# Three row blocks of scores in one stretch, the decays' products of two head pairs in one stretch, two later steps of groups: a hybrid decoder layer on one Trainium2 core

## The chip, the cores and the metric

The kernel runs on one core of one Trainium2 chip. The core has a matrix engine (PE in the profile, with its weight loads, PEld), a vector engine (DVE), a scalar engine (ACT), a general engine (POOL) and a sync engine (SP), which all run their own instruction queues in order and wait for each other by semaphores. The metric is the time of one execution on the device in microseconds (us), the median of several runs. Before the change it is 1290.15 us, the median of three runs (1289.37 to 1290.36).

## The reference

The input is x, 512 tokens of width 1024, and a memory of 256 tokens of the same width. The layer is a feed-forward half step, a mixer, a cross-attention into the memory, and a second feed-forward half step, each behind an RMS norm and added to x. All is in float32. The change lies in the mixer, which has two kinds of heads behind one input projection and ahead of one output projection:

```python
z, xbc, dt_raw, q, k, v = split_sizes(h @ w_in, IN_SIZES)
xbc = silu(causal_dwconv(xbc, conv_w, conv_b))          # 4 taps
# SSD: 16 heads of 64 in 4 groups, chunks of 128 tokens
decay = exp(where(causal, la_cum[l] - la_cum[s], -inf))
y_diag = einsum('bclsg,bclsgr,bcsgrp->bclgrp', cb, decay, xdt)
y_off = einsum('bclgn,bcgrpn,bclgr->bclgrp', cc, prev, exp(la_cum))
y = (y_diag + y_off + d_skip * xh) * silu(z)            # then an RMS norm by group
# differential attention: 8 heads, 2 components of 64, values of 128, query blocks of 128
p = softmax(q @ k.T * scale + bias, causal)             # for both components
o = (p[0] - lam * p[1]) @ v                             # then an RMS norm by head
out = concatenate([y_ssd, y_attn]) @ w_out
```

`y_diag` is what the tile `py` holds, and `y_off` what `pf` holds. A query block of row i sees the keys of blocks 0 to i alone, so its scores are 128 by 128(i+1).

## The kernel before

The whole layer is one program. Activations are kept with features on the partitions and 512 tokens along the free axis. Every float32 weight and activation is split into a high part and a low remainder (`split_into`, L153), and a product is made of three passes of matmuls: high by high, low by high, high by low. The dense projections are runs of 24 matmuls of 128x512, written `pq<-hnh,wh` and the like, into a bank of PSUM; the tile gets its name from what it holds (`pq`, `pk` queries and keys of a head, `pxbc` and `pz` inputs of the SSD groups, `pm` output projection, `pcv` values of the memory).

PSUM has eight banks here in two pools of four: `acc` for the dense projections, and `aux` for all that the heads and groups do beside them (`ps` scores, `pt` turned weights, `po` outputs of a head, `ptk` and `pot` two transposes of these, `pcb`, `pxt`, `pbt`, `pst`, `pf`, `py` and `nps`, `nrow` of a group). A new tile takes the bank that has been in use for the longest time, and its first matmul waits for the last reader of that bank.

The order of the work is set in two steps. A class `Order` runs generators: the dense projections step matmul by matmul, and the heads (`head`, L766) and groups (`group`, L928) are spawned beside them and resume when a clock, which every matmul moves on by an estimate of its time, has passed what they yielded. These delays stand in a table `W` (`hs` between the steps of a head, `gd`, `gt`, `gy`, `gq`, `gn` between those of a group). A scheduler of the framework then sets the order on PE, DVE and ACT from that program; the order of SP and POOL is that of the program.

In `head` (L766) the scores of the four row blocks are made by `scores`: for each block three passes over two components, each component a matmul on 64 of PE's rows (`64*128` in the profile), both at once, into a bank for each component. A read on DVE (L787, a custom operation that scales, adds the bias and keeps the minimum, followed by a small read of that minimum `mn`) and an exponential on ACT (L788) follow for each component. `combine(i)` makes the difference of the two components on DVE (L796, L798, L799), and `turn(j)` transposes the columns of key block j into `pt`, which is then split into `wt` on ACT and DVE. `po` sums the values, ACT copies it (`of`), and PE transposes it (`ptk`). Before the change a head runs `scores(3)`, `scores(2)` one step later, and `scores(1, 0)`, both into one pair of banks, one step after that.

In `group` (L928) the last part (from L982) runs twice, once for each pair of heads j: the decays come from a row on ACT (L989 to L993), then `pf` takes three matmuls and `py` eight, of 128x128, four chunks by two heads, each on 64 of PE's columns (`128*64` in the profile). DVE then makes `y` (L1008, L1009), and with `z` (L1017) the gated output, whose squares (`ysq`) go to a sum over tokens, an inverse root on POOL (`ncol`, L368) and back to a row (`nrow`). `decays(g + 1, j)` fetches the row for the next group into the tile that the group has just read. The taps of the convolution (L901) run on DVE beside that and are the last readers of a bank of `pxbc`.

## Time and profile before

| what | us |
| --- | --- |
| median of 3 runs | 1290.15 |
| the profiled execution | 1289.51 |
| its span, first to last instruction | 1287.7 |
| PE busy | 1275.9 (99%) |
| DVE busy | 969.3 (75%) |
| ACT busy | 708.2 (55%) |
| mixer with its heads and groups | about 375 to 840 of the span |
| PE busy from 375 to 840 | 464.38 of 465 |

A row of a timeline reads: start, duration, engine, line, operation, tile written and tiles read, rows by columns of PE that are used, shape and number of like instructions one after the other, and in brackets how long the engine had been idle and what it then waited for. Matmuls overlap their neighbours, so the time that one takes is best read from the starts of the rows. The clock of PE was granted at 0.997 of full speed over the execution.

### The profile page before, as it was taken

The page shows a single profiled execution, that of the slowest core. Times are in us where ns is not written, and L with a number is a line of the kernel's source. Part 1 is how long each engine was busy: PE and PEld are TensorE (multiplying, and loading weights), DVE is VectorE, ACT ScalarE, POOL GpSimd, SP SyncE. Part 2 cuts the span into 40 slices and gives each one's busy share as a digit, 9 for nine tenths or more (in the row PEclk, how much of TensorE's full clock was granted, in tenths as well). Part 3 has the DMA queues.
Part 4 walks back from the last instruction along what each step waited for, and adds up shares of the span by engine and source line. Part 5 has one row for each costly group of instructions (what it writes and reads, how often), then busy time and mean ns, then how long its engine had stood idle before and what let it go on. Part 6 is the DMA issues. An engine that isn't in the chain of part 4 may idle for free.

```text
span 1287.7 us, 20009 instructions
## 1 busy us (share of the span) xinstructions
PE 1275.9 (99%) x7673; PEld 1115.9 (87%) x7673; DVE 969.3 (75%) x1547; ACT 708.2 (55%) x1207; POOL 111.6 (9%) x135
## 2 busy tenths in 40 slices
PE   9999999999999999999999999999999999999996
PEld 7889998998988788877888878888899899989995
DVE  6988898788875786657768697546668878877886
ACT  7545564566654564446654566434475546545554
POOL 1001010002201011101102011020001000000000
PEclk9999999999999999999999999999999999999998
DMA  9468677789865436753376457593259776666662
GB/s 338 104 173 209 180 204 203 217 217 238 284 205 159 128 74 191 214 173 84 96 224 199 137 150 241 197 229 99 69 160 243 207 222 177 193 190 187 186 202 87
DMA packets 69695, 234.70 MB, mean 182 GB/s; under 512 B 8144, under 2 KB 9568, under 8 KB 69248
## 3 DMA queue, kind: packets, MB, share of 16 engines
q1 hardware_dynamic: 53504, 181.12, 41.9%
q0 software_dynamic: 13456, 45.67, 19.8%
q10 hardware_dynamic: 2640, 6.65, 1.6%
q8 instruction: 60, 0.98, 0.3%
q14 instruction: 35, 0.29, 0.1%
HBM read 231.25 MB, written 48.29 MB: 217 GB/s over the span
## 4 chain that ended last, share of the span: by engine, by line
PE 88%; issue 9%; ACT 1%; POOL 1%; DMA 1%; DVE 1%; POOLq 0%; DVEq 0%; ACTq 0%
PE qb L244 13%; PE pm L146 9%; PE qe L244 9%; PE qa L244 8%; PE ob L1328 7%; PE oa L1328 5%; PE oe L1328 4%; PE pk L146 3%; PE pv L146 3%; PE pq L146 3%; PE pcq L146 3%; PE pxbc L146 3%; PE pck L146 2%; PE pa L146 2%; PE pg L146 2%
## 5 line engine op out<-in xcount | busy, mean ns | idle before, releaser
L155 ACT ACTIVATE wh<-wr 128x1024 fp32r<-128x1024 f32 (+1 forms) x245 | 251.2, 1028 | 223.4 <-PE qe L244 31.0
L156 DVE TENSOR_TENSOR wl<-wr,wh 128x1024 fp32r<-128x1024 f32 (+1 forms) x245 | 290.0, 1186 | 74.6 <-ACT wh L155 60.2
L1308 ACT ACTIVATE wh<-wr 128x1024 fp32r<-128x1024 f32 (+1 forms) x74 | 72.8, 984 | 65.9 <-PE ob L1328 17.4
L1317 DVE TENSOR_TENSOR wl<-wr,wh 128x1024 fp32r<-128x1024 f32 (+1 forms) x74 | 82.7, 1126 | 12.9 <-ACT wh L1308 11.0
L788 ACT ACTIVATE ec<-ec,mn 128x512 f32<-128x512 f32 (+3 forms) x64 | 35.3, 554 | 21.9 <-DVE mn L787 21.9
L787 DVE CUSTOM_DVE_ANT_0 ec<-ps,bias 128x512 f32<-128x512 f32 (+3 forms) x64 | 28.1, 487 | 16.2 <-PE ps L146 16.1
L368 POOL TENSOR_TENSOR ncol<-nv,mhalf 128x4 f32<-128x4 f32 (+1 forms) x9 | 11.4, 1271 | 299.8 <-DVE nv L366 299.8
L901 DVE SCALAR_TENSOR_TENSOR conv<-pxbc,par,conv 128x511 f32<-128x511 f32 (+2 forms) x48 | 35.8, 745 | 1.9 <-ACT conv L897 1.3
L253 POOL DMA_DIRECT2D wr<-in_f2q x11 | 9.7, 879 | 306.1 <-DMA wr<-in_f2q 230.4
L146 PE MATMUL pxbc<-hnl,wh 128*128 128x512 f32 x128 | 35.6, 405 | 0.0
L146 PE MATMUL pxbc<-hnh,wh 128*128 128x512 f32 x128 | 34.7, 398 | 0.0
L146 PE MATMUL pxbc<-hnh,wl 128*128 128x512 f32 x128 | 32.5, 393 | 0.0
L456 DVE TENSOR_TENSOR gate<-qb,row 128x512 f32<-128x512 f32 x19 | 13.1, 692 | 20.3 <-PE qb L244 20.3
L146 PEld LDWEIGHTS pxbc<-hnh,wl 128*128 128x128 f32 x128 | 23.7, 188 | 5.2 <-issue 0.2
L146 PEld LDWEIGHTS pxbc<-hnl,wh 128*128 128x128 f32 x128 | 23.1, 188 | 4.9 <-issue 0.6
L146 PEld LDWEIGHTS pxbc<-hnh,wh 128*128 128x128 f32 x128 | 23.4, 189 | 4.6 <-issue 0.3
L253 POOL DMA_DIRECT2D wr<-in_f1q x16 | 14.0, 872 | 152.3 <-DVE wl L156 44.6
L457 ACT ACTIVATE gate<-gate 128x1024 f32<-128x1024 f32 x19 | 20.1, 1057 | 10.9 <-DVE gate L456 10.9
L146 PE MATMUL pv<-wh,hnh 128*128 128x512 f32 x64 | 25.4, 398 | 0.0
L146 PE MATMUL pv<-wh,hnl 128*128 128x512 f32 x64 | 25.1, 393 | 0.0
L155 ACT ACTIVATE s24h<-s 128x512 fp32r<-128x512 f32 x30 | 18.8, 627 | 9.0 <-DVE s L214 9.0
L155 ACT ACTIVATE s31h<-s 128x512 fp32r<-128x512 f32 x30 | 18.7, 624 | 7.3 <-DVE s L212 4.2
(472 smaller groups left out, 3506.3 us busy)
## 6 DMA issues: line engine op xcount, KB each, us to landing
wr<-in_f2q SPq DMA_DIRECT2D x44, 512.0 KB, 4.3
wr<-in_f1q SPq DMA_DIRECT2D x40, 512.0 KB, 4.7
wr<-in_f1b SPq DMA_DIRECT2D x23, 512.0 KB, 6.3
isum<-in_f2q SPq DMA_DIRECT2D x22, 512.0 KB, 6.2
wr<-isum SPq DMA_DIRECT2D x22, 512.0 KB, 3.5
wsum<-in_f2b SPq DMA_DIRECT2D x20, 512.0 KB, 5.6
wr<-wsum SPq DMA_DIRECT2D x20, 512.0 KB, 4.4
wr<-in_f1q POOLq DMA_DIRECT2D x16, 512.0 KB, 6.8
```

Of the source, the lines that this page charges most:

```text
L146: newest_mm[:] = [nc.tensor.matmul(out, w, x, start=start, stop=stop).ins]
L155: S.activation(hi, src, AF.Copy),
L156: V.tensor_tensor(lo, src, hi.bitcast(F32), ALU.subtract),
L244: newest_mm[:] = [nc.tensor.matmul(out, w_[:, wc], xs[kp][which][x_], start=first and j == 0 and f == 0 and kp == 0, stop=j == 2 and kp == ...
L253: last_sum[:] = [G.dma_start(raw, m, accum_op=ALU.add).ins]
L457: S.activation(gate, gate, AF.Silu)
L787: V.tensor_tensor_reduce(out=ec[:, :n], in0=ps[c][:, parts[i]], in1=bias[:, T - n :], scale=0.125, scalar=3e38, op0=ALU.add, op1=ALU.min, ...
L788: S.activation(ec[:, :n], ec[:, :n], AF.Exp, bias=mn, scale=-1.0, accum_out=sm[c][:, i : i + 1])
L901: V.scalar_tensor_tensor(y[:, d:], ps[:, : T - d], par[:, cw + j : cw + j + 1], y[:, d:], ALU.mult, ALU.add)
L1308: recent[:] = [S.activation(hi[:, i * n : (i + 1) * n], r, AF.Copy).ins for i, r in enumerate(raw)]
L1317: recent.append(V.tensor_tensor(lo[:, ns], r, hi[:, ns].bitcast(F32), ALU.subtract).ins)
L1328: newest_mm[:] = [nc.tensor.matmul(ps, a_[:, ts], b_[:, ws], start=first and k == 0 and j == 0, stop=k == n - 1 and j == 2, skip_group_che ...
```

## The change

Three things change, all in the mixer. `scores` takes groups of blocks, each group with its own pair of banks, and makes all matmuls ahead of all reads: block 3 alone first, as before, then blocks 2 and 0 in one pair of banks and block 1 in another, in one stretch, where block 2 stood alone. Nothing of the scores is left for the third step. In groups 0 to 2 the `py` of the first pair of heads waits until the `pf` of the second pair has been made, and both `py` stand in one stretch; the reads of both, and both transfers of decays, follow. In group 3 each pair has its own, as before. The step ahead of the second `pf` is later by 0.5 in groups 2 and 3, where it was so in group 2, and the row of the norm (`nrow`) is taken up 2.6 later in groups 0 to 2 and 1.4 later in group 3, where it was 1.1.

```diff
...
         es, w0, w1 = {}, {}, {}
         sm = [small("sm", 4) for _ in range(2)]
 
-        def scores(*blocks):
-            ps = [aux("ps") for _ in range(2)]
-            parts, to = {}, 0
-            for i in blocks:
-                n = P * (i + 1)
-                parts[i] = slice(to, to + n)
-                to += n
-                for j, (u, w) in enumerate(((0, 0), (0, 1), (1, 0))):
-                    for c in range(2):
-                        pc = slice(64 * c, 64 * c + 64)
-                        mm(ps[c][:, parts[i]], q[u][pc, i * P : (i + 1) * P], kq[w][pc, :n], j == 0, j == 2)
-            for i in blocks:
+        def scores(*pairs):
+            parts = {}
+            for blocks in pairs:
+                ps, to = [aux("ps") for _ in range(2)], 0
+                for i in blocks:
+                    n = P * (i + 1)
+                    parts[i] = [p_[:, to : to + n] for p_ in ps]
+                    to += n
+                    for j, (u, w) in enumerate(((0, 0), (0, 1), (1, 0))):
+                        for c in range(2):
+                            pc = slice(64 * c, 64 * c + 64)
+                            mm(parts[i][c], q[u][pc, i * P : (i + 1) * P], kq[w][pc, :n], j == 0, j == 2)
+            for i in parts:
                 n = P * (i + 1)
                 es[i] = []
                 for c in range(2):
                     ec = s2("ec", shape=(P, n))
                     mn = small("mn", 1, bufs=8)
-                    V.tensor_tensor_reduce(out=ec[:, :n], in0=ps[c][:, parts[i]], in1=bias[:, T - n :], scale=0.125, scalar=3e38, op0=ALU.add, op1=ALU.min, accum_out=mn)
+                    V.tensor_tensor_reduce(out=ec[:, :n], in0=parts[i][c], in1=bias[:, T - n :], scale=0.125, scalar=3e38, op0=ALU.add, op1=ALU.min, accum_out=mn)
                     S.activation(ec[:, :n], ec[:, :n], AF.Exp, bias=mn, scale=-1.0, accum_out=sm[c][:, i : i + 1])
                     es[i].append(ec)
 
...
                 w0[j], w1[j] = s2("wt", R32, (P, n)), s2("wt", R32, (P, n))
             split_into(w0[j], w1[j], pt[:, :n])
 
-        scores(3)
+        scores((3,))
         yield W["hs"]
-        scores(2)
+        scores((2, 0), (1,))
         combine(3)
         yield W["hs"]
-        scores(1, 0)
         combine(2)
         turn(3)
         yield W["hs"]
...
             if c < 2:
                 yield W["gs"]
         yz = []
+        def off_diagonal(j, e2):
+            pf = aux("pf")
+            with behind(list(newest_mm)):
+                for c in range(1, 4):
+                    mm(pf[:, c * P : (c + 1) * P], st[c - 1][:, j * P : (j + 1) * P], ct[:, c * P : (c + 1) * P], True, True)
+            V.scalar_tensor_tensor(e2[:, P:], pf[:, P:], 0.5, e2[:, P:], ALU.mult, ALU.mult)
+
+        def diagonal(j, rs, e2):
+            py = aux("py")
+            with behind(list(newest_mm)):
+                for c in range(4):
+                    for hh in (1, 0):
+                        pp = slice(64 * hh, 64 * hh + 64)
+                        mm(py[pp, c * P : (c + 1) * P], xdt[c // 2][:, c % 2, (2 * j + hh) * 64 : (2 * j + hh + 1) * 64], rs[hh][:, c], True, True)
+            return py
+
+        def joined(j, py, e2):
+            if g < 3:
+                decays(g + 1, j)
+            dsk = dskh[:, 2 * g + j : 2 * g + j + 1]
+            y = s2("y")
+            V.scalar_tensor_tensor(y, xs[j], dsk, py, ALU.mult, ALU.add)
+            V.tensor_tensor(y[:, P:], y[:, P:], e2[:, P:], ALU.add)
+            dump(f"y_{2*g+j}", y)
+            yz.append(y)
+
+        together = []
         for j in range(2):
             rs = rows_of.pop((g, j))
-            py = aux("py")
             e2 = s2("e2")
             for hh in range(2):
                 hd = 4 * g + 2 * j + hh
...
                     S.activation(r[:, c], r[:, c], AF.Relu, bias=cum[:, c, hd : hd + 1], scale=-1.0)
                 S.activation(r, r, AF.Exp, scale=-1.0)
                 V.tensor_tensor(r, r, cbm, ALU.mult)
-            yield W["gd"] + (W["gt"] if j == 0 else 0.5 if g == 2 else 0.0)
-            pf = aux("pf")
-            with behind(list(newest_mm)):
-                for c in range(1, 4):
-                    mm(pf[:, c * P : (c + 1) * P], st[c - 1][:, j * P : (j + 1) * P], ct[:, c * P : (c + 1) * P], True, True)
-                for c in range(4):
-                    for hh in (1, 0):
-                        pp = slice(64 * hh, 64 * hh + 64)
-                        mm(py[pp, c * P : (c + 1) * P], xdt[c // 2][:, c % 2, (2 * j + hh) * 64 : (2 * j + hh + 1) * 64], rs[hh][:, c], True, True)
-            if g < 3:
-                decays(g + 1, j)
-            dsk = dskh[:, 2 * g + j : 2 * g + j + 1]
-            V.scalar_tensor_tensor(e2[:, P:], pf[:, P:], 0.5, e2[:, P:], ALU.mult, ALU.mult)
-            y = s2("y")
-            V.scalar_tensor_tensor(y, xs[j], dsk, py, ALU.mult, ALU.add)
-            V.tensor_tensor(y[:, P:], y[:, P:], e2[:, P:], ALU.add)
-            dump(f"y_{2*g+j}", y)
-            yz.append(y)
+            yield W["gd"] + (W["gt"] if j == 0 else 0.5 if g > 1 else 0.0)
+            off_diagonal(j, e2)
+            together.append((j, rs, e2))
+            if j or g == 3:
+                pys = [diagonal(*one) for one in together]
+                for (j_, _, e), py in zip(together, pys):
+                    joined(j_, py, e)
+                together.clear()
             yield W["gy"]
         while len(zs) < 2:
             yield 1.0
...
         yield W["gq"] + (1.2 if g == 2 else 0.0)
         pn = yield from sums_by_token(sq[0], 4)
         rh = inv_rms_cols(pn, 4, 4.0 / (4 * 256), 4.0 * EPS)
-        pr = yield from row_of(rh, 4, W["gn"] + 1.1)
+        pr = yield from row_of(rh, 4, W["gn"] + (2.6 if g < 3 else 1.4))
         for j in range(2):
             n = 2 * g + j
             V.scalar_tensor_tensor(yz[j], yz[j], par[:, C_SSD + n : C_SSD + n + 1], pr, ALU.mult, ALU.mult)
```

The scheduler moves instructions with that. Three places show it. The first is DVE in the second head: a row with L787 (before) or L788 (now) is the read of scores, or of its minimum; the two `ps` are the components. Before:

```order
L787 ISA ec_4719,mn_4720<-ps_4711,bias_4096 128x384
L787 ISA mn_4720 128x1
L787 ISA ec_4723,mn_4724<-ps_4712,bias_4096 128x384
L787 ISA mn_4724 128x1
L796 RECIPROCAL rc_4727<-sm_4673 128x1
L798 SCALAR_TENSOR_TENSOR rl_4729<-sm_4672,nlam,rc_4727 128x1
L799 SCALAR_TENSOR_TENSOR ec_4682<-ec_4686,rl_4729,ec_4682 128x512
L796 RECIPROCAL rc_4775<-sm_4673 128x1
L798 SCALAR_TENSOR_TENSOR rl_4777<-sm_4672,nlam,rc_4775 128x1
L799 SCALAR_TENSOR_TENSOR ec_4719<-ec_4723,rl_4777,ec_4719 128x384
L787 ISA ec_4759,mn_4760<-ps_4745,bias_4096 128x256
```

Now:

```order
L797 RECIPROCAL rc_4757<-sm_4673 128x1
L799 SCALAR_TENSOR_TENSOR rl_4759<-sm_4672,nlam,rc_4757 128x1
L800 SCALAR_TENSOR_TENSOR ec_4682<-ec_4686,rl_4759,ec_4682 128x512
L788 ISA ec_4733,mn_4734<-ps_4711,bias_4096 128x384
L788 ISA mn_4734 128x1
L788 ISA ec_4737,mn_4738<-ps_4712,bias_4096 128x384
L788 ISA mn_4738 128x1
L788 ISA ec_4741,mn_4742<-ps_4711,bias_4096 128x128
L788 ISA mn_4742 128x1
L788 ISA ec_4745,mn_4746<-ps_4712,bias_4096 128x128
L788 ISA mn_4746 128x1
L788 ISA ec_4749,mn_4750<-ps_4725,bias_4096 128x256
```

The combination of block 3 stood behind the reads of block 2 and stands ahead of them now, and the reads of blocks 0 and 1 follow at once.

The second is PE in the third head, around the outputs `po` of that head's predecessor. Before, the end of `po` and what follows:

```order
L146 MATMUL po_4926<-wt_4864,vh_4519 128x384
L146 MATMUL po_4926<-wt_4823,vh_4523 128x256
L146 MATMUL po_4926<-wt_4782,vh_4527 128x128
L146 MATMUL po_4926<-wt_4881,vh_4515 128x512
L146 MATMUL ps_4942<-kh_4795,qh_4698 128x256
L146 MATMUL ps_4943<-kh_4795,qh_4698 128x256
L146 MATMUL ps_4942<-kl_4796,qh_4698 128x256
L146 MATMUL ps_4943<-kl_4796,qh_4698 128x256
```

Now, the end of the scores and the beginning of `po`:

```order
L146 MATMUL ps_4898<-kh_4795,ql_4699 128x256
L146 MATMUL ps_4899<-kh_4795,ql_4699 128x256
L146 MATMUL pk_4939<-hnh_3833,wh_4942 128x512
L146 MATMUL pk_4939<-hnh_3857,wh_4942 128x512
L146 MATMUL pk_4939<-hnh_3886,wh_4942 128x512
L146 MATMUL pk_4939<-hnh_3909,wh_4942 128x512
L146 MATMUL po_4950<-wt_4880,vh_4515 128x512
L146 MATMUL po_4950<-wt_4863,vh_4519 128x384
```

The scores of the 256 columns stood behind `po` and stand ahead of it now, with four matmuls of `pk` between; `po` takes the bank of a `ps`.

The third is DVE where the third group (g = 2) ends; `hm` is a split of the memory, `conv` are taps of one `pxbc`, `y` the outputs of a pair of heads. Before:

```order
L160 SCALAR_TENSOR_TENSOR hm_7819<-mem_7682,par,hm_7819 128x256
L901 SCALAR_TENSOR_TENSOR conv_7808<-pxbc_7719,par,conv_7808 128x510
L1008 SCALAR_TENSOR_TENSOR y_7846<-th_1559_7513,dskh,py_7753 128x512
L901 SCALAR_TENSOR_TENSOR conv_7808<-pxbc_7719,par,conv_7808 128x509
L1009 TENSOR_TENSOR y_7846<-y_7846,e_1615_7754 128x384
L1017 TENSOR_TENSOR y_7846<-y_7846,th_1575_7587 128x512
L1021 TENSOR_TENSOR ysq_7851<-ysq_7851,ysq_7854 128x512
L160 SCALAR_TENSOR_TENSOR hm_7857<-mem_7704,par,hm_7857 128x256
```

Now:

```order
L160 SCALAR_TENSOR_TENSOR hm_7804<-mem_7681,par,hm_7804 128x256
L901 SCALAR_TENSOR_TENSOR conv_7793<-pxbc_7718,par,conv_7793 128x510
L1002 SCALAR_TENSOR_TENSOR y_7841<-th_1548_7454,dskh,py_7821 128x512
L1002 SCALAR_TENSOR_TENSOR y_7846<-th_1559_7511,dskh,py_7830 128x512
L1003 TENSOR_TENSOR y_7841<-y_7841,e_1592_7638 128x384
L1003 TENSOR_TENSOR y_7846<-y_7846,e_1611_7738 128x384
L1033 TENSOR_TENSOR y_7841<-y_7841,th_1560_7520 128x512
L1033 TENSOR_TENSOR y_7846<-y_7846,th_1575_7587 128x512
L901 SCALAR_TENSOR_TENSOR conv_7793<-pxbc_7718,par,conv_7793 128x509
L156 TENSOR_TENSOR wl_8006<-wr_8003,wh_8005 128x512
L1037 TENSOR_TENSOR ysq_7851<-ysq_7851,ysq_7854 128x512
```

All six operations on both `y` stand between the second and the third tap of that convolution, where there was one. On PE the two `py` of groups 0 and 1 stand together now, 16 matmuls in a row; those of group 2 do not: six matmuls of `pxbc` and 21 of `pz` lie between.

## The prediction

> **What bounds the kernel now.** I read the page first: busy shares, then the chain that ended last.
>
> ```profile
> span 1287.7 us, 20009 instructions
> PE 88%; issue 9%; ACT 1%; POOL 1%; DMA 1%; DVE 1%; POOLq 0%; DVEq 0%; ACTq 0%
> ```
>
> The chain is PE itself, 88%, and 9% "issue", in which PE waited for nobody. So the time changes only if PE gets less to do or has to stand still. The profiled run took 1289.51 us, 0.64 less than the median shown; I sum against the former. Next, what PE waits for in the mixer (view of waits, PE, 375 to 840):
>
> ```profile
> PE nrow L150 <- POOL ncol L368: 0.5, 1, 0.5
> ```
>
> One wait in 465 us. The mixer is packed without a gap, so every wait that the change makes is paid in full, and every saved stretch is gained in full. Last I read the timelines around the moved places: PE and DVE in the second head (427 to 434), PE, DVE and ACT in the third (441 to 449), all three at the end of group 2 (743 to 753).
>
> **What the change removes: switches of PE's shape.** PE, second head:
>
> ```profile
> 427.09 0.61 PE L146 MATMUL pk<-hnh,wh 128*128 128x512 f32 x2
> 427.63 0.44 PE L146 MATMUL ps<-kh,qh 64*128 64x384 f32 x2
> 427.91 0.34 PE L146 MATMUL ps<-kl,qh 64*128 64x384 f32 x2
> 428.08 0.34 PE L146 MATMUL ps<-kh,ql 64*128 64x384 f32 x2
> 428.35 1.65 PE L146 MATMUL pk<-hnh,wh 128*128 128x512 f32 x6
> 429.84 1.52 PE L146 MATMUL pk<-hnl,wh 128*128 128x512 f32 x6
> 432.13 0.33 PE L150 MATMUL pt<-ident,ec 128*128 128x128 f32 x1
> 432.21 0.71 PE L146 MATMUL pk<-hnl,wh 128*128 128x512 f32 x2
> 432.76 2.00 PE L146 MATMUL pk<-hnh,wl 128*128 128x512 f32 x8
> ...
> 744.09 1.98 PE L146 MATMUL pz<-hnl,wh 128*128 128x512 f32 x8
> 745.91 1.05 PE L146 MATMUL pcb<-th,th 128*128 128x128 f32 x8
> 748.63 1.07 PE L146 MATMUL pm<-yah,wh 128*128 128x512 f32 x4
> ```
>
> A dense step is (745.91−744.09)/8 = 0.227. The rest is the price of a stretch of 64 rows. Ahead of it two dense steps take 0.54 instead of 0.45 (+0.09); its first pass takes 0.28 where the second takes 0.17 (+0.11); its last takes 0.27 (+0.10); six dense steps behind it take 1.49 instead of 1.36 (+0.12). Together 0.42 for going there and back. From 427.09 to 432.76 stand 16 dense steps (3.63) in 5.67: the two stretches and a `pt` cost 2.04. Merged they cost 2.04 − 0.42 = 1.62, without the `pt`, which stood in the second stretch for 0.08 (432.13 to 432.21), about 1.56. By itself that `pt` costs about 0.06 more than there (estimated; none to 0.12). So 0.36 is saved in each head, for eight heads **−2.9**.
>
> The two products of decays:
>
> ```profile
> 679.05 1.09 PE L146 MATMUL py<-th,xdt 128*64 128x128 f32 x16
> ```
>
> Sixteen half-width matmuls lie between two switches. I price these like those above, 0.42, less a little for the `pf` that stood beside one of them: 0.4 for a merged pair. The new order joins them in groups 0 and 1 only; in group 2 they remain apart, in group 3 by intent. **−0.8**; bounds 0 (the switch back to dense costs nothing for half columns) and −0.9.
>
> **What it adds in the heads: waits for banks.** `aux` has four banks. A merged stretch fills all four at once, so the next tile needs what DVE has to read first, and on DVE the reads now stand behind the combination of block 3. DVE, second head:
>
> ```profile
> 429.09 0.55 DVE L787 CUSTOM_DVE_ANT_0 ec<-ps,bias 128x384 f32<-128x384 f32 x1
> ...
> 430.04 0.16 DVE L796 RECIPROCAL rc<-sm 128x1 f32<-128x1 f32 x1
> ...
> 431.16 0.16 DVE L796 RECIPROCAL rc<-sm 128x1 f32<-128x1 f32 x1
> ...
> 432.23 0.42 DVE L787 CUSTOM_DVE_ANT_0 ec<-ps,bias 128x256 f32<-128x256 f32 x1
> ...
> 432.92 0.28 DVE L787 CUSTOM_DVE_ANT_0 ec<-ps,bias 128x128 f32<-128x128 f32 x1
> ...
> 433.13 0.28 DVE L787 CUSTOM_DVE_ANT_0 ec<-ps,bias 128x128 f32<-128x128 f32 x1
> ```
>
> Two reads of 384 take 0.95 (to 430.04), the combination 1.12 (to 431.16), a read of 128 takes 0.21. Now the combination starts at 429.09, and the bank of blocks 2 and 0 is free at 429.09+1.12+0.95+0.21+0.08+0.05 = 431.5 (0.08 the read of the minimum, 0.05 the handover). PE wants it for the lone `pt`: it reaches that after the merged stretch and eight dense steps, 427.54+1.56+1.82 = 430.9. Wait 0.58. Behind it all of PE waits; the same order returns in the fifth head: **+1.1** for the two.
>
> The third head, where `po` comes from the head before it:
>
> ```profile
> 442.22 0.44 PE L146 MATMUL ps<-kh,qh 64*128 64x384 f32 x2
> 442.94 2.12 PE L146 MATMUL pk<-hnh,wh 128*128 128x512 f32 x8
> 445.35 0.74 PE L146 MATMUL po<-wt,vh 128*128 128x512 f32 x4
> 447.35 0.39 PE L146 MATMUL ps<-kh,qh 64*128 64x256 f32 x2
> ```
>
> ```profile
> 441.89 1.23 DVE L156 TENSOR_TENSOR wl<-wr,wh 128x1024 fp32r<-128x1024 f32 x1 [0.56 <-PE pq L146]
> 443.04 0.68 DVE L156 TENSOR_TENSOR wt<-pt,wt 128x512 fp32r<-128x512 f32 x1
> 443.63 0.55 DVE L787 CUSTOM_DVE_ANT_0 ec<-ps,bias 128x384 f32<-128x384 f32 x1
> ```
>
> ```profile
> 444.23 0.62 ACT L788 ACTIVATE ec<-ec,mn 128x384 f32<-128x384 f32 x1 [0.75 <-DVE mn L787]
> 447.46 0.60 ACT L843 ACTIVATE of<-po 128x512 f32<-128x512 f32 x1 [1.92 <-PE po L146]
> 448.75 0.51 ACT L788 ACTIVATE ec<-ec,mn 128x256 f32<-128x256 f32 x1 [0.70 <-DVE mn L787]
> ```
>
> Three waits follow one another. First, the fourth of the new banks held the last `pt`, whose `wt` ends at 443.04+0.68 = 443.72, held up by `wl`, which itself waited for PE. PE wants it at 442.94−0.10 (the 384 columns done, no switch) + about 0.27 (128 columns) = 443.1: **0.64**. Second, PE goes on at 443.78, needs 0.57 for the rest of the stretch and its exit and 1.01 for four dense steps with their first, and wants the bank of blocks 2 and 0 for `po` at 445.36. DVE has from 443.63 on 1.12, 0.95 and 0.29 to do, 446.0: **0.7**. Third, `ptk` waits for `of`, and that on ACT now stands behind six exponentials: 443.63+1.12+0.47+0.1 = 445.3, then 2×0.61+2×0.51+2×0.4 (the last pair estimated) = 448.35, with `of` and a handover 449.05. PE has twelve `po` (2.0, by 445.35 to 447.35), a `pt` and three dense steps from 446.05 on: 448.85. **0.2 to 0.3**; before, the second stretch of scores covered it, 1.0 long. That is 1.66 in this head. In the sixth more dense work lies ahead of `po`, which leaves 0.35 of the second wait: 1.25. The fourth and seventh head have the second and the third wait, about 0.5 and 0.27: 1.6 for the two. The first and the last have small ones of about 0.2 each. Heads together 1.1+1.66+1.25+1.6+0.4 = **+6.0**; from below 1 (only what one head in three shows), from above 8 (three waits in every head from the second to the seventh would be 10, less what a wait earlier in the head forgives).
>
> A rule of the Trainium skill speaks against the merged stretch. "TensorEngine Tiling (Array Packing)", section "PSUM Bottleneck", says that matmuls on parts of the array become faster while the reading of PSUM does not, and that the reading may become the bottleneck. By that rule alone the sum would have the excess of the reads, +4.0 (second rival), in place of +6.0. The trace of before neither shows nor excludes it, since its stretches never fill more than two banks at once.
>
> **What it adds in the groups.** Group 2, ACT and DVE:
>
> ```profile
> 744.52 0.63 ACT L1019 ACTIVATE ysq<-y 128x512 f32<-128x512 f32 x1 [1.65 <-PE pz L146]
> ```
>
> ```profile
> 743.24 0.48 DVE L160 SCALAR_TENSOR_TENSOR hm<-mem,par,hm 128x256 fp32r<-128x256 f32 x1
> 743.63 0.74 DVE L901 SCALAR_TENSOR_TENSOR conv<-pxbc,par,conv 128x510 f32<-128x510 f32 x1
> 744.29 0.74 DVE L1008 SCALAR_TENSOR_TENSOR y<-th,dskh,py 128x512 f32<-128x512 f32 x1
> 744.95 0.74 DVE L901 SCALAR_TENSOR_TENSOR conv<-pxbc,par,conv 128x509 f32<-128x509 f32 x1
> 745.61 0.55 DVE L1009 TENSOR_TENSOR y<-y,e 128x384 f32<-128x384 f32 x1
> 746.19 0.69 DVE L1017 TENSOR_TENSOR y<-y,th 128x512 f32<-128x512 f32 x1
> ...
> 752.36 0.69 DVE L875 TENSOR_TENSOR x<-x,pm 128x512 f32<-128x512 f32 x1 [0.25 <-PE pm L146]
> ```
>
> The `pm` that starts at 748.63 takes the bank of that `pxbc`, which the last tap (744.95) frees early. Now the split `hm` ahead of the second tap takes the place on ACT of the `ysq` that waited for `pz` until 744.52, and between second and third tap stand six operations on `y`: 744.52+0.5 (ACT) +0.4 (`hm`) +0.66 (tap) +2×0.66+2×0.5+2×0.61 (`y`) +0.74 (tap) +0.05 = 750.4. **+1.75** in front of `pm`. Behind it the next `pm` is handed the bank of a `pm` whose update on DVE (0.69, row 752.36) it must wait for: end of the last matmul 0.39+0.04, update, handover 0.05, less a step that PE needs anyway, **+0.9**; before, the order of banks gave it another. `nrow` is asked for later by the new delay, but only three dense steps of four remain ahead of it: **+0.2**. The moved transfers of decays wait for the second `py`; in groups 0 and 1 that is near, and the next group needs them tens of us later: 0.
>
> Sum: −2.9 −0.8 +6.0 +1.75 +0.9 +0.2 = +5.15; 1289.51+5.15 = 1294.7, against the median 1295.3. I say **1295.0**. About 0.2% (2.6 us) is what a measurement of this kernel can tell from no change.
>
> **The rivals.** *Switches alone (faster).* If DVE takes the reads ahead of the combination wherever they are ready, or the banks come free in another order, no `pt` and no `po` waits, and the savings of 3.7 stand: 1286.4. For it speaks that DVE is idle a quarter of the time (table above); against it, that the queue runs in the written order, and that DVE had no gap from 441.89 to 444.1 in the third head (rows above). It decides once the waits fall below 1 in all. 12%. *Reads alone (no change).* The six reads of a merged stretch take 0.95+0.69+0.42 = 2.06 on DVE by the rows of the second head, the stretch 1.56 on PE; only that excess of 0.5 is lost in each of eight heads, +4.0, and the `pm` of group 2 gets another bank: 4.0−3.7 = +0.3, 1290.5. For it, PE's waits overlap where one forgives the next; against, the three waits in the third head have three different causes. 15%. *Late weights (slower still).* DVE and ACT, late by 0.6 in a head, hand the next weights over late; `wl` in the third head has 0.56 in hand. If half a us more is lost in five heads: 1297.5. 13%. *Nothing merged.* In group 2 the order shows it to be so, and the sum has it.
>
> **How the numbers follow.** Forecast 60%: 1295.0, its own range 1292.5 to 1297. Slower by over 0.2% needs above 1292.7: nearly all of the forecast and the last rival, 0.72. Within 0.2%: the second rival and the low end of the forecast, 0.16. Faster 0.12. The range leaves out the first rival and the tail of the third: 1289 to 1297.5.
>
> **What would show it.** In the timeline of PE in the second head, one stretch of `ps` with 384, 128 and 256 columns, 1.3 to 1.4 us to its exit, and a `pt` eight dense steps later with some 0.6 of idle time put down to DVE `mn`; in the third head three gaps, before `ps` of 256, `po` and `ptk`. In group 2 a gap of 1.75 ahead of `pm`, put down to `conv`. The waits of PE from 375 to 840 should sum to about 9 instead of 0.5. A sum under 4 means that the order on DVE doesn't hold PE, and the forecast is wrong. If PE's waits are as said and the time is not, the switch is mispriced.

## The result, and the profile after

The changed kernel takes 1296.94 us, the median of five runs (1296.26 to 1297.33), beside 1290.36 for the kernel before (1289.37 to 1290.4): a ratio of 1.0052, 95% interval 1.004 to 1.0065. It is slower by 6.6 us. Run once more (`change_again` below) it took 1296.39, a ratio of 1.0048, 1.0036 to 1.0061. The prediction said 1295.0, within 1289 to 1297.5, and slower. The trace of the changed kernel read below is of an execution of 1297.33 us.

The page of the changed kernel, its span and its chain:

```profile
span 1295.5 us, 20011 instructions
PE 72%; issue 9%; DVE 2%; ACT 1%; DMA 1%; POOL 1%; POOLq 0%; DVEq 0%; ACTq 0%
```

PE still sets the end. DVE has 2% of the chain where it had 1%; PE's share falls from 88% to 72%, and the shares listed no longer fill the span, so this view does not show where the time went. What PE waits for in the mixer (view of waits, PE, 375 to 850; total, times, longest) was one line of 0.5 before, and is now this:

```profile
PE pm L146 <- ACT ysq L1035: 1.7, 1, 1.7
PE po L146 <- ACT ec L789: 1.5, 3, 0.6
PE nrow L150 <- POOL ncol L368: 0.8, 1, 0.8
PE pm L146 <- DVE x L875: 0.8, 1, 0.8
PE pt L150 <- DVE mn L788: 0.7, 2, 0.3
PE ps L146 <- DVE wt L156: 0.6, 2, 0.3
```

These are the waits that the prediction named: `pt`, `ps` and `po` in the heads, two `pm` and `nrow` in the third group. They sum to 6.1, where the prediction gave about 9 for this view, and `ptk`, which it named too, isn't among them. The view counts only the time in which the profile has PE empty. The row of a dense matmul lasts 0.39 us while the next one starts after 0.227, so the loss read from the starts is larger, by about 0.16 to 0.2 at each of these waits and by 0.33 at `ps`, and waits shorter than that don't show at all.

The second head on PE:

```profile
429.15 0.61 PE L146 MATMUL pk<-hnh,wh 128*128 128x512 f32 x2
429.70 0.44 PE L146 MATMUL ps<-kh,qh 64*128 64x384 f32 x2
...
430.32 0.22 PE L146 MATMUL ps<-kh,qh 64*128 64x128 f32 x2
...
430.61 0.34 PE L146 MATMUL ps<-kh,qh 64*128 64x256 f32 x2
...
431.11 1.66 PE L146 MATMUL pk<-hnh,wh 128*128 128x512 f32 x6
432.61 0.62 PE L146 MATMUL pk<-hnl,wh 128*128 128x512 f32 x2
433.57 0.33 PE L150 MATMUL pt<-ident,ec 128*128 128x128 f32 x1 [0.34 <-DVE mn L788]
```

and on DVE:

```profile
431.15 0.15 DVE L797 RECIPROCAL rc<-sm 128x1 f32<-128x1 f32 x1
...
432.26 0.55 DVE L788 CUSTOM_DVE_ANT_0 ec<-ps,bias 128x384 f32<-128x384 f32 x1
...
433.43 0.08 DVE L788 DVE_READ_ACCUMULATOR2_ANT mn<- 128x1 f32 x1
```

The three blocks stand in one stretch of 1.41 (429.70 to 431.11). From 429.15 to the end of the eight dense steps behind it, 432.61+2×0.227 = 433.06, lie ten dense steps and the stretch: 3.91−2.27 = 1.64, where 1.56 was reckoned. `pt` starts at 433.57, 0.51 later than it could, 0.06 behind the end of the read of the minimum (433.43+0.08). The combination of block 3 stands in front of the reads and takes 1.11 (431.15 to 432.26), as forecast.

The third head:

```profile
445.50 0.33 PE L146 MATMUL ps<-kh,qh 64*128 64x256 f32 x1
446.13 0.38 PE L146 MATMUL ps<-kh,qh 64*128 64x256 f32 x1 [0.30 <-DVE wt L156]
...
446.68 1.21 PE L146 MATMUL pk<-hnh,wh 128*128 128x512 f32 x4
448.50 0.84 PE L146 MATMUL po<-wt,vh 128*128 128x512 f32 x4 [0.61 <-ACT ec L789]
```

```profile
445.39 0.69 DVE L156 TENSOR_TENSOR wt<-pt,wt 128x512 fp32r<-128x512 f32 x1
...
448.27 0.08 DVE L788 DVE_READ_ACCUMULATOR2_ANT mn<- 128x1 f32 x1
```

The two components of a block run at once, yet here their starts are 0.63 apart: the second waits for the bank that `wt` leaves at 446.08. Then `po` waits. The profile puts that down to an exponential on ACT, which `po` doesn't read; by the program the last read of the bank that `po` takes is the one on DVE that ends with its minimum at 448.35, 0.15 ahead of `po`. The trace does not decide between the two, as the exponential follows the reads; either way the order on DVE sets it, since `reads_first` below, where only an order on DVE is set by hand, does away with the wait. `ptk` waits too short a time for the view: it starts at 451.42, 0.05 behind the end of `of` (450.77+0.60) and 0.20 later than the three dense steps ahead of it would let it (450.54+3×0.227 = 451.22).

The third group, PE and then DVE:

```profile
752.67 1.07 PE L146 MATMUL pz<-hnh,wl 128*128 128x512 f32 x4
755.42 1.16 PE L146 MATMUL pm<-yah,wh 128*128 128x512 f32 x4 [1.68 <-ACT ysq L1035]
...
758.49 0.73 PE L146 MATMUL pm<-yah,wl 128*128 128x512 f32 x2
760.01 1.19 PE L146 MATMUL pm<-yah,wh 128*128 128x512 f32 x4 [0.78 <-DVE x L875]
```

```profile
750.02 0.49 DVE L160 SCALAR_TENSOR_TENSOR hm<-mem,par,hm 128x256 fp32r<-128x256 f32 x1 [0.90 <-ACT hm L159]
...
751.08 1.40 DVE L1002 SCALAR_TENSOR_TENSOR y<-th,dskh,py 128x512 f32<-128x512 f32 x2
752.39 1.02 DVE L1003 TENSOR_TENSOR y<-y,e 128x384 f32<-128x384 f32 x2
753.33 1.29 DVE L1033 TENSOR_TENSOR y<-y,th 128x512 f32<-128x512 f32 x2
754.53 0.74 DVE L901 SCALAR_TENSOR_TENSOR conv<-pxbc,par,conv 128x509 f32<-128x509 f32 x1
```

This is the row of work of the forecast, in its order: `hm` late behind ACT, a tap (left out above), three pairs of operations on `y`, the last tap, and `pm` 0.15 behind that tap's end (754.53+0.74 = 755.27). Again the profile names another, `ysq` on ACT, which ends at the same time; `pm` reads nothing of it. The second `pm` starts 0.06 behind the update of `x` that it waits for (759.26+0.69 = 759.95).

Where the time went is best seen from the starts of the dense matmuls, which come in nearly the same order in both kernels (at 23 of 3285 places another stands): how much later the n-th of them starts than in the kernel before, at some points of the mixer (time in the kernel before). Two of the experiments below stand beside it.

| at | what lies before it | change | scores_only | groups_only |
| --- | --- | --- | --- | --- |
| 375 | what the change doesn't touch | 1.98 | 1.13 | 0.50 |
| 438 | first two heads | 2.36 | 1.56 | 0.52 |
| 500 | third and fourth head | 4.24 | 3.42 | 0.50 |
| 528 | group 0 | 3.90 | 3.42 | 0.16 |
| 575 | fifth head | 4.20 | 3.72 | 0.16 |
| 664 | sixth to eighth head | 5.52 | 5.00 | 0.17 |
| 720 | group 1 | 4.99 | 5.00 | -0.36 |
| 752 | group 2 up to its second wait of `pm` | 7.76 | 5.00 | 2.40 |
| 850 | the rest | 7.86 | 5.10 | 2.47 |

The change loses 5.88 in the mixer (7.86−1.98). The 1.98 ahead of it is no part of it; what it is stands in the last section.

### The profile page after: what moved, and what is told of

Read it like the earlier page. It is cut to its first block, busy times and chain, and to the rows that moved or that the text cites. A ratio compares the mean times of both kernels' runs of the same rounds, so it can differ in the third digit from the quotient of the medians.

```text
span 1295.5 us, 20011 instructions
## 1 busy us (share of the span) xinstructions
PE 1277.7 (99%) x7673; PEld 1117.7 (86%) x7673; DVE 965.8 (75%) x1547; ACT 708.8 (55%) x1207; POOL 110.7 (9%) x135
## 4 chain that ended last, share of the span: by engine, by line
PE 72%; issue 9%; DVE 2%; ACT 1%; DMA 1%; POOL 1%; POOLq 0%; DVEq 0%; ACTq 0%
PE qb L244 10%; PE pm L146 8%; PE qe L244 7%; PE qa L244 7%; PE ob L1344 6%; PE oa L1344 4%; PE pv L146 3%; PE pcq L146 3%; PE oe L1344 3%; PE pq L146 3%; PE pxbc L146 3%; PE pk L146 3%; PE pck L146 2%; PE pcv L146 2%; PE po L146 1%
## 5 line engine op out<-in xcount | busy, mean ns | idle before, releaser
L788 DVE CUSTOM_DVE_ANT_0 ec<-ps,bias 128x512 f32<-128x512 f32 (+3 forms) x64 | 27.5, 486 | 14.1 <-PE ps L146 14.1
L155 ACT ACTIVATE wt<-pt 128x256 fp32r<-128x256 f32 (+3 forms) x32 | 13.9, 433 | 17.4 <-PE pt L150 17.2
```

The costliest lines, as they stand in the source:

```text
L155: S.activation(hi, src, AF.Copy),
L788: V.tensor_tensor_reduce(out=ec[:, :n], in0=parts[i][c], in1=bias[:, T - n :], scale=0.125, scalar=3e38, op0=ALU.add, op1=ALU.min, accum_o ...
```

## The experiments

### The parts apart: scores_only and groups_only

```diff
 # scores_only, against the kernel before: the edit of scores() and its calls alone
-        scores(3)
+        scores((3,))
         yield W["hs"]
-        scores(2)
+        scores((2, 0), (1,))
         combine(3)
         yield W["hs"]
-        scores(1, 0)
 # groups_only, against the kernel before: all other edits of the change
```

> The merged scores as in the change, the groups and all delays as before. Theory 'banks': the heads' waits for banks are the larger part of the loss, whatever the groups do; in the trace of the change the dense steps of the mixer are late by 2.4 us more behind the first four heads and by 1.6 more behind the last four, net of the switches saved: +4.0, about 1294.4 us, and in the second head a wait of `pt`, in the third one each of `ps`, `po` and `ptk`. Rival 'meeting': the heads lose little by themselves and the loss comes from late reads meeting late groups: +2 or less, 1292.4 or less. Rival 'groups': the heads gain what their switches save, 1287.5.

Measured: 1294.08 us, ratio 1.003 (1.0019 to 1.0042). In the trace 3.97 us are lost in the mixer (last column but one of the table, 5.10−1.13). Its waits in the heads (beside them `nrow` waits 0.4, as before, and a `py` 0.2):

```profile
PE po L146 <- ACT ec L789: 1.7, 4, 0.6
PE pt L150 <- DVE mn L788: 0.7, 2, 0.3
PE ps L146 <- DVE wt L156: 0.6, 2, 0.3
```

> The groups' products, the steps and the delays as in the change, the scores as before. Theory 'banks': groups 0 and 1 gain 0.4 each; group 2 loses 1.75 ahead of the one `pm` and 0.95 ahead of the next, and little at `nrow`: +1.8, about 1292.2 us. Rival 'meeting': +1 or less, as the taps are only late behind late heads. Rival 'groups': all of the loss, +6.

Measured: 1292.05 us, ratio 1.0017 (1.0008 to 1.0026); in the trace 1.97 (2.47−0.50).

The parts sum to 5.94 in the traces, the change to 5.88. So they don't meet, and the two rivals of a meeting or of one part alone fall. Two thirds of the loss come from the heads and one third from the groups: the third loses 2.8, and groups 0 and 1 give 0.9 back.

### Group 2 as before: two_groups

```diff
-            if j or g == 3:
+            if j or g > 1:
```

> The change, with groups 2 and 3 both by pairs of heads, so that only groups 0 and 1 have both products in one stretch. Theory 'banks': both waits of `pm` in the third group go, 1.75 and 0.95, and no merged stretch is lost, as the order had not joined them there: 2.7 less than the change, about 1294.2 us. Rival 'stretch': the two waits move to another tile of that group and the time stays at 1297.

Measured: 1293.69 us, ratio 1.0027 (1.0017 to 1.0038), 3.3 below the change; by the dense starts of the two traces it is 2.4. The waits of `pm` are gone and no other has grown:

```profile
PE po L146 <- ACT ec L789: 1.5, 3, 0.6
PE nrow L150 <- POOL ncol L368: 0.8, 1, 0.8
PE pt L150 <- DVE mn L788: 0.7, 2, 0.3
PE ps L146 <- DVE wt L156: 0.6, 2, 0.3
```

The first `pm` starts without a wait behind the last `pz`:

```profile
750.96 2.07 PE L146 MATMUL pz<-hnh,wl 128*128 128x512 f32 x8
752.87 1.07 PE L146 MATMUL pm<-yah,wh 128*128 128x512 f32 x4
```

Nothing else is touched by hand, and the `py` of that group stand apart in both: the wait comes from the six operations on `y` in one go, not from the matmuls.

### The delays alone: delays_only

```diff
-            yield W["gd"] + (W["gt"] if j == 0 else 0.5 if g == 2 else 0.0)
+            yield W["gd"] + (W["gt"] if j == 0 else 0.5 if g > 1 else 0.0)
...
-        pr = yield from row_of(rh, 4, W["gn"] + 1.1)
+        pr = yield from row_of(rh, 4, W["gn"] + (2.6 if g < 3 else 1.4))
```

> The two later steps alone: 0.5 ahead of the second `pf` in group 3 too, and the row of the norm taken up 2.6 later in groups 0 to 2 and 1.4 in group 3 in place of 1.1; scores and products as before. Theory: nothing that waits is moved but `nrow` of the third group, which has waited 0.5 for `ncol` and waits 0.7 to 0.9 as one dense step less lies ahead of it: +0.3, 1290.5 us, no difference that can be measured. Rival: the later row is what hands the third group its waits of `pm`, +2.7, 1293.

Measured: 1290.89 us, ratio 1.0004 (0.9995 to 1.0013): no difference that can be told. `nrow` waits 0.8 where it waited 0.5, as in the change; the later request doesn't help, since PE has a dense step less ahead of it.

### The price of a switch: four_stretches

```diff
                         mm(ps[c][:, parts[i]], ...)
+                if i != blocks[-1]:
+                    yield 0.2
             for i in blocks:
...
-        scores(1, 0)
+        yield from scores(1, 0)
```

> The kernel before, but the scores of blocks 1 and 0 in two stretches with one dense step between; same banks, same reads, behind the second of them. It doubles the disputed saving with the sign turned: a switch there and back more in each of eight heads. Theory: 0.42 each, less what the read of the small block is late, +2.4 to +3.4, about 1293 us. Rival 'switch is cheap' (the extra time of a stretch lies in its small matmuls and would stay in a merged one): +0.8 or less.

Measured: 1293.06 us, ratio 1.0023 (1.0015 to 1.0032). The experiment did less than it was meant to: the order on PE split the stretch in four heads only, the third, fourth, sixth and seventh, by the transposes `ptk` rather than by a dense step, and left the others whole (28 stretches of scores instead of 24). The third head:

```profile
449.19 0.39 PE L146 MATMUL ps<-kh,qh 64*128 64x256 f32 x2
...
449.54 0.28 PE L146 MATMUL ps<-kh,ql 64*128 64x256 f32 x2
449.95 0.66 PE L150 MATMUL ptk<-ident,of 128*128 128x128 f32 x4
...
451.11 1.62 PE L146 MATMUL pk<-hnl,wh 128*128 128x512 f32 x6
```

In its trace the mixer loses 3.07. That isn't the price of four switches alone, since `ptk` now stands ahead of the end of `of` and waits in all four heads: 1.1 in the view for the fourth and the seventh, and too little for the view in the others. In the third head 1.92 pass from the first `ps` to the dense steps, where it was 1.36 in the kernel before (447.35 to 448.71). In the kernel before, the row behind a stretch of `ps` starts 0.20 behind its last pass (447.98 to 448.18), so `ptk` could have started at 449.74 and started 0.21 later. That leaves 0.35 for the switch; the same reckoning gives 0.3 to 0.35 in the other three heads. A switch isn't cheap, but it costs somewhat less than the 0.42 forecast.

### The order on DVE: reads_first

```diff
+                    reads[:] = [V.tensor_tensor_reduce(..., accum_out=mn).ins]
...
         scores((2, 0), (1,))
-        combine(3)
+        with behind(list(reads)):
+            combine(3)
```

> The change, with the combination of block 3 kept behind the reads of blocks 2, 0 and 1 on DVE; nothing else is moved by hand. Theory 'banks, set by the order on DVE': the banks come free 1.1 us earlier in each head, so `po` and `ptk` in the third, fourth, sixth and seventh head wait less; but the combinations come later, and `pt`, which transposes what they make, waits for them instead, in the second, fourth, fifth and seventh head about 0.4 to 0.6 each. On balance 1 to 1.5 us less than the change, about 1295.6 us, with `pt` behind DVE `ec` among the waits in place of `po`. Rival 'pace': DVE is busy with the same work, so the time doesn't change, 1296.9. Rival 'order alone': every wait of the heads goes, 1291.

Measured: 1293.82 us, ratio 1.0029 (1.0018 to 1.0041); in its trace the mixer loses 3.86 instead of 5.88.

```profile
PE pm L146 <- ACT ysq L1038: 1.7, 1, 1.7
...
PE pt L150 <- DVE ec L802: 0.7, 2, 0.3
PE ps L146 <- DVE wt L156: 0.6, 2, 0.3
```

Not an instruction fewer, and 2.0 us less lost in the mixer (3.1 less by the medians): the waits of `po` are gone altogether, those of `pt` now name the combination `ec` in place of `mn`, and those of `ps`, which wait for `wt`, and of `pm` are untouched. The pace of the reads is the same in both, so "pace" falls. The gain is larger than the 1 to 1.5 expected, since `pt` waits in two heads and not in four. "Order alone" falls too: the heads still wait for what the late combination makes, and for `wt`.

### The rest moved round the merged scores: tuned, tuned_late, tuned_heads, tuned_2

```diff
 # tuned, against the change
         scores((3,))
-        yield W["hs"]
-        scores((2, 0), (1,))
+        yield 2.5
         combine(3)
-        yield W["hs"]
+        yield W["hs"] - 3.1
+        scores((2,), (1, 0))
+        yield W["hs"] + 0.5
...
-        yield W["hs"]
+        yield W["hs"] - 0.7
         turn(1)
-        yield W["ht"]
+        yield W["ht"] - 1.4
         turn(0)
-        yield W["hs"] + (0.8 if hd % 4 == 3 else 0.0)
+        yield W["hs"] + (1.9 if hd % 4 == 3 else 1.1)
...
-        yield W["hv"]
+        yield W["hv"] + 1.1
...
-        yield W["hp"]
+        yield W["hp"] - 0.2
...
-            yield W["gd"] + (W["gt"] if j == 0 else 0.5 if g > 1 else 0.0)
+            yield W["gd"] + (W["gt"] if j == 0 else 0.0)
-            if j or g == 3:
+            if j or g > 1:
-        pr = yield from row_of(rh, 4, W["gn"] + (2.6 if g < 3 else 1.4))
+        pr = yield from row_of(rh, 4, W["gn"] + (3.0 if g == 2 else 1.4))
```

> The merged scores with the rest of the head moved round them: the combination of block 3 gets a step of its own ahead of the second scores, the small block shares a pair of banks with block 1, `po` and `ptk` come 1.1 later, the last two turns earlier; in the groups both products in one stretch for the first two groups alone, no extra step in the third, and its row of the norm taken up 1.9 later. All matmuls, reads and switches of the change but for the third group. Theory 'banks': with the waits gone the switches saved stand: -2.9 in the heads, -0.7 in the groups, some 0.3 lost to the small waits that stay, and the wait of `nrow` gone: 1287.0 us, faster than both kernels, with no wait of `pt`, `po`, `ps` or `ptk` above 0.3. Rival 'pace of the reads' (a merged stretch costs what its six reads on DVE take longer than its matmuls): 4 us of loss remain, 1291 or more.

Measured: 1287.69 us, ratio 0.9978 (0.997 to 0.9987): faster than both kernels. Its waits in the mixer are two:

```profile
PE pcum L146 <- DVE dth L698: 0.3, 1, 0.3
PE py L146 <- DVE th L1020: 0.2, 1, 0.2
```

With the same three blocks in one stretch, the same reads on DVE and as many stretches of scores as the change (16, where the kernel before has 24), the loss of the change is a gain. The reads are the same, so their pace was not the price. Several steps were moved at once here; what each of them is worth was not tested apart, but for the one that follows.

```diff
 # tuned_late, against tuned
-        yield 2.5
-        combine(3)
-        yield W["hs"] - 3.1
+        yield W["hs"] - 0.6
         scores((2,), (1, 0))
+        combine(3)
```

> The same, but the combination of block 3 directly behind the second scores, as in the change. Theory 'banks, set by the order on DVE': `pt` waits about 1.2 in the second and in the fifth head, behind the combinations, and the other waits stay away: 3.1 more, about 1290.1 us. Rival 'pace': the place of the combination is worth nothing, 1287.

Measured: 1290.49 us, ratio 1.0003 (0.9994 to 1.0012), 2.8 above `tuned`. The wait came back in the two heads named, and nearly as long (tuned_late, waits, and PE in the second head):

```profile
PE pt L150 <- DVE ec L800: 2.3, 2, 1.1
```

```profile
434.21 0.33 PE L150 MATMUL pt<-ident,ec 128*128 128x128 f32 x1 [1.14 <-DVE ec L800]
```

Beside it `ptk` waits 0.3 once, which was not expected. The place of one combination of 1.1 us on an engine that is busy for 75% of the time is worth all of the gain.

```diff
 # tuned_heads, against tuned: the groups as before the change
-            if j or g > 1:
+            if j or g > -1:
-        pr = yield from row_of(rh, 4, W["gn"] + (3.0 if g == 2 else 1.4))
+        pr = yield from row_of(rh, 4, W["gn"] + 1.1)
 # and the extra 0.5 in group 2 back
```

> The tuned heads alone, the groups with each pair's products by itself and all delays as before. It gives the price of the switches saved in the heads, without waits: if a stretch less is worth 0.36 in each of eight heads, -2.9, and some 0.3 to 1 is lost to small waits at the beginning and by the groups' meeting other tiles: 1287.5 to 1288.7 us. If a switch is cheap: 1290. And what `tuned` has beyond it is the groups' part, 1 to 1.7.

Measured: 1288.96 us, ratio 0.999 (0.9981 to 0.9999). It lies just above the range given. The heads gain about 1.3 (1.0 by the dense starts), and the groups' part of `tuned` about as much (1.7 by the dense starts). Where a part of the rest of the 2.9 went, the timeline of `tuned` shows: each `pot` is four transposes and costs 0.445 above the dense steps about it, but three of the eight cost 0.68 to 0.79, like this one:

```profile
608.73 0.66 PE L150 MATMUL pot<-ident,on 128*128 128x128 f32 x4
```

They wait for `on`, too short a time to be listed as idle. So the step ahead of `pot` was set later:

```diff
 # tuned_2, against tuned
-        yield W["hp"] - 0.2
+        yield W["hp"] + 0.2
```

> The tuned kernel with the step ahead of `pot` 0.4 later. In the trace of the tuned one four transposes of `pot` at 0.445 each but three of them take 0.68, 0.68 and 0.79, as they wait for `on`, 0.8 in all. Theory: two dense steps more ahead of each `pot` hide that, and the time falls by 0.8 to 1286.9 us, three `pot` at 0.445 again. Rival: what follows on the banks gets late in its place, and the time stays at 1287.7 or rises.

Measured: 1285.97 us, ratio 0.9967 (0.9955 to 0.998). In its trace the mixer gains 3.6 against the kernel before, `tuned` 2.7: the 0.8 forecast is there, and the rest of the 1.7 by which the medians differ lies ahead of the mixer or isn't explained. The three `pot` now cost as much as the other five.

It is the fastest version here, 4.2 us below the kernel before and 10.4 below the change, both measured beside it.

### The change again: change_again

The same kernel, unchanged.

> The change once more, beside the other two on one chip. In its first trace the dense steps of the mixer fall back by 5.9 us against the kernel before, and another 1.3 is lost in the first 6 us of the program, ahead of anything that the change touches, where other kernels lose between 0 and 1.2. Theory: the change itself costs 5.9, 1296.1 us give or take the start. Rival: it costs 6.6 or more, something outside the mixer, 1297.

Measured: 1296.39 us, ratio 1.0048 (1.0036 to 1.0061). In its trace the mixer loses 5.92 (from 2.06 at 375 to 7.98 at 850), and 0.95 had been lost in the first 6 us. So the change costs about 5.9; what the traces show above that lies ahead of it.

## Why the prediction was right

The sign, the places and most of the sizes held. Point by point:

- **What bounds.** Every wait in the mixer was paid in full: parts and whole agree to 0.1, and no later slack gave any of it back.
- **Switches.** −2.9 was forecast for the heads, and this is the term that was mis-sized. The merged stretch took 1.64 in the second head instead of 1.56, and by the same reckoning 1.61 to 1.64 in the four others in which no wait falls into it (first, fourth, fifth, seventh). A lone `pt` costs 0.12 to 0.13 (the traces of the change and of `tuned`), close to the estimate. So a head saves about 2.04−1.64−0.12 = 0.28 and not 0.36; `four_stretches` gives 0.3 to 0.35 for a switch instead of 0.42. Eight heads would save about 2.3. `tuned_heads` got 1.3 of it (1.0 by the dense starts); of the 3.6 of `tuned_2` the heads have 2.0. In the first head nothing was earned: the stretch of blocks 1 and 0 had stood there directly ahead of other work of an odd shape (`pdk`, 32 rows) and shared its way back with that; this is read from the timeline and wasn't tested.
- **The products of decays.** −0.8 forecast for groups 0 and 1; the table shows −0.34 (3.90−4.24) and −0.53 (4.99−5.52). That group 2 isn't merged was read from the order, and was so.
- **Waits in the heads.** +6.0 forecast. The heads lose 3.9 net (`scores_only`) where 3.1 had been forecast. Most of the 0.8 between is the saving that was taken too large; with a saving of about 2 in place of 2.9 the waits themselves come out near the 6.0. The first two heads lose 0.43 where about 0 had been forecast, the first one for want of its saving. In the second head `pt` waited 0.51 (0.58 forecast), in the third `ps` 0.63 between its components (0.64), `po` 0.8 against the four dense steps behind the stretch, 446.68+4×0.227+0.1 = 447.7 (0.7), `ptk` 0.20 (0.2 to 0.3). The three terms of the third head as written give about 1.6 and not quite the 1.66 that was summed.
- **The third group.** +1.75 and +0.9 forecast; the first `pm` came 1.84 late (755.42 against 752.67+4×0.227 = 753.58), the second 0.96 by the dense starts. `two_groups` took both away with one condition. `nrow` waits 0.8 instead of 0.5, where +0.2 was forecast.
- **The sum, and what was to show it.** 5.15 forecast, 5.88 measured in the mixer. The view of waits shows 6.1 and not about 9; that 9 was a sum of losses read from starts, which the view shows smaller. The loss of 5.88 and the savings, about 2 in the heads and 0.9 in the groups, put the waits near 9 by the starts. The median lies 1.9 above the 1295.0, at the edge of the forecast's own range. The mixer accounts for 0.7 of that; the rest lies ahead of the mixer, as far as the profiled executions show, and the prediction had no term for it. That it did not carry the time out of the range is luck.
- **The rivals.** "Switches alone" would need no wait above 1 in all; there were 6. `tuned_2` comes to 1285.97, near the 1286.4 reckoned for it, but that is another program, and its gain is made up otherwise: 2.0 in the heads, 0.9 in groups 0 and 1, the rest behind them. "Reads alone" had 4.0 of loss less 2.9 saved for the heads, 1.1 net, where 3.9 net were measured, and `reads_first` and `tuned` keep all the reads and lose less or nothing. The rule of the Trainium skill behind it ("TensorEngine Tiling (Array Packing)", section "PSUM Bottleneck") names the place, the emptying of PSUM, but here it is when a bank is read that counts, not for how long. "Late weights" was not seen: no wait for weights stands in the view.

Left open are the small waits of the first two heads, one by one, what released `po` and the first `pm` (DVE by the program, ACT by the profile), and why `reads_first` spares the fourth and the seventh head the wait of `pt`.

## What to carry to other kernels

When PE has no gap, the price of merging work on it is read from who empties its banks: write down for each bank the last reader and what stands ahead of that reader on its engine, and compare that time with the moment at which PE asks for the bank next. Merging stretches of matmuls pays (about 0.3 us each here), but here only after what stands ahead of the reads had been moved to another place; one combination of 1.1 us undid a gain of 2.5. Operations that were one by one and now come in a burst hold up what stood between them, and the tap of a convolution that frees a bank is such a thing.

## What the hardware showed that was not expected

The first matmuls of the program run at a slower pace, and how long that lasts differs from one execution to the next. Kernel before, then the change, PE:

```profile
1.44 3.40 PE L355 MATMUL init<-ones_r 128*128 128x512 f32 x8 [1.44 <-DVE ones_r L351]
4.90 1.18 PE L146 MATMUL pa<-hmh,wah 128*128 128x512 f32 x4
5.92 1.09 PE L146 MATMUL pa<-hml,wah 128*128 128x512 f32 x4
```

```profile
1.44 3.78 PE L355 MATMUL init<-ones_r 128*128 128x512 f32 x8 [1.44 <-DVE ones_r L351]
5.02 2.01 PE L146 MATMUL pa<-hmh,wah 128*128 128x512 f32 x4
6.83 1.46 PE L146 MATMUL pa<-hml,wah 128*128 128x512 f32 x4
```

In the kernel before the eight `init` take (4.90−1.44)/8 = 0.43 a step and the next four (5.92−4.90)/4 = 0.255; in the change it is (5.02−1.44)/8 = 0.45 and (6.83−5.02)/4 = 0.45. By the starts of single matmuls a step is 0.427 until about 4.3 us in the one and 7.6 in the other (2.9 and 6.2 behind the first matmul), and soon 0.23 behind that; all other traces begin at 0.427 too and change between about these two times. The view of the clock prints 1.00 for the first 10 us of both, but the records of the granted clock begin at 4.27 and at 7.62 us, so the slow stretch has no record. At 6.4 us the change is behind by 1.27, and the other traces by −0.17 (`tuned_2`), −0.09 (`reads_first`), 0.49 (`groups_only`) and up to 1.21 (`two_groups`); kernels with the same program up to there. The second execution of the change is behind by 0.95, so the kernel alone doesn't set it. The Trainium skill, "TensorE: Matmul & The Clock Gate", section "Part 1: The HAM clock gate", says that the first few us run at half clock and that how many matmuls this catches varies by the run, with 0.427 from start to start for 512 columns; the slow rows here agree with that. With it, single executions here differ by up to 1.4 us without a cause in the kernel, a quarter of the loss studied here.

Ahead of the mixer also lies a stop of 0.6 to 1.1 at about 191 us that some executions have and others don't (0.68 in the change, none in `scores_only`); in the trace of the change `ob` waits there for a copy on ACT.

The second thing is how the view of waits names and sizes. It put `po` down to an exponential and `pm` to a square on ACT, which neither of them reads, where by the program DVE held the bank; no run here moves the one without the other. And it showed 0.34 of a loss of 0.51. The starts of the dense matmuls, compared between two kernels, give the size of a loss.
